# First layer of a three-layer network on one core: input loads moved behind their readiness, four gate buffers, elementwise products moved from GpSimd to VectorE

## The chip, the core and the metric

The kernel runs on one core of one Trainium2 chip. The metric is the device time of one execution in microseconds (us), lower is better. The core's engines are TensorE (PE; its weight loads are listed apart as PEld), VectorE (DVE), ScalarE (ACT), GpSimd (POOL) and SyncE (SP). They run side by side and wait for each other by semaphores. Transfers are issued by SP and by ScalarE here, each of which has a row of transfers of its own; the names SPq and ACTq in a row mean the issuing side of those engines.

## The reference

The network has three layers on x of 512 tokens by 1024 features: a time-mixing layer of the RWKV-7 kind, a layer of forgetting attention, and a hybrid sparse-attention layer, each followed by an MLP. The change lies in the first layer's time mixing, cut here to what it computes (h is the normalised input; 16 heads of 64):

```python
xs = h[None] + xx[None] * mu[:, None, None, :]      # six mixes of h and the token before
rkv = einsum('pbtd,pde->pbte', stack([x_r, x_k, x_v]), w_rkv)
w = -softplus(-(w0 + tanh(x_w @ w1) @ w2)) - 0.5;  decay = exp(-exp(w))
a = sigmoid(a0 + (x_a @ a1) @ a2)
g = sigmoid(x_g @ g1) @ g2                          # the gate
...
def step(S, inp):                                   # once per token, S is 64 x 64 per head
    sa = einsum('bhvk,bhk->bhv', S, -kk_t)
    S = S * w_t + sa[..., None] * b_t[:, :, None, :] + v_t[..., None] * k_t[:, :, None, :]
    return S, einsum('bhvk,bhk->bhv', S, r_t)
y = (y - mean) * rsqrt(var + GN_EPS)                # per head
y = y * lnx_w + lnx_b
y = (y + bonus) * g
return y @ w_o                                      # added to x by the caller
```

## The kernel before

Matrix products of the large layers are taken as three products of high and low parts: an operand is split into a rounded high part (`wh`, a ScalarE copy) and the remainder (`wl`, a subtraction on VectorE or GpSimd). The kernel is written as generators which are advanced in turn; a scheduler then orders each engine's instructions from those of all generators, and puts in the semaphores. Buffers come from pools by tag, so a tile waits until an older tile of its tag is no longer read. The first layer lasts until about 500 us of the trace; after it come its MLP and the other two layers.

The first layer's core goes through the 512 tokens in chunks of 64, and its work in halves: `T2` is the half of the tokens (256 each), `hs` the half of the heads, and `tt` one of four tiles of 128 tokens.

- `rwkv_gate` makes the gate: it mixes x again (`xh` buffers), multiplies by two small matrices, and writes 8 tiles `gst` (128x512) to memory, each by a ScalarE copy out of PSUM (L1147) and a store issued by ScalarE (L1148).
- `rwkv_prep` stores the scaled keys and queries into `dQ` in memory. `prepare(T2)` in `rwkv_core` reads them back (`KBg` at L1306, `Qd` and `Qe` at L1310), multiplies them (L1315) into 8 matrices `G` of 128x16x128, and masks each product (128x512, 32 in all). In the first half VectorE masks straight from PSUM; in the second half ScalarE copies every second product out of PSUM (L1320) and GpSimd masks it (L1322).
- `rwkv_inverse` inverts 32x32 triangles for all heads in 31 steps of two VectorE instructions (L1263, L1265), once for each half.
- `chain(hs)` carries the state through 8 chunks. After each tile of tokens `rwkv_post` normalises the result `y` (L1531 to L1542) with one product on GpSimd (L1540); TensorE then transposes it (L1546).
- `weight(k, ...)` loads the 8 row blocks of the output matrix and splits them, two 128x512 pieces each: high part on ScalarE (L1439), low part `wo` on GpSimd (L1440).
- `out(tt)` loads the layer's input x again for one tile of tokens (L1448, two loads of 128x4x128, 256 KB each), multiplies by the output matrix, and adds.

Of the kernel before, what the change touches and what calls it, by code (L numbers as in the profile page):

```python
# [9 lines left out]
F32 = mybir.dt.float32  # L10
# [3 lines left out]
ALU = mybir.AluOpType  # L14
# [4 lines left out]
P = 128  # L19
D = 1024  # L20
T = 512
# [10 lines left out]
class Net:  # L32
# [1072 lines left out]
    def rwkv_gate(self, e):  # L1105

        nc, a, pool, fv = self.nc, self.a, e["p7"], e["p2"]
        w = self.load_w(a["rw_g1"], 1280)
        Ms = (P, 32)
        ps = [self.bank("t") for _ in range(2)]  # L1110
        for m in range(NK):
            h, d = self.rwkv_again(e, pool, m, pool, "xd", 2)
            nc.vector.scalar_tensor_tensor(d, d, self.v("mu5", m), h[:, 1:], op0=ALU.mult, op1=ALU.add)
            xh, xl = self.split(pool, d, "xg", 2, lpool=m % 2 == 0)
            o = 160 * m
            for p, M in zip(ps, Ms):
                self.mm3(p[:M], w[0][:, o:o + M], w[1][:, o:o + M], xh, xl, m == 0, m == NK - 1)
                o += M
            yield
        sh, sl = [pool.tile([P, T], F32R, name=n) for n in ("sgh", "sgl")]  # L1120
        st = pool.tile([96, T], F32R, name="sgt")
        for i, M in enumerate(Ms):
            t = pool.tile([P, T], F32, tag="xd", bufs=2, name=self.nm("sg"))[:M]
            nc.scalar.activation(t, ps[i][:M], AF.Tanh, scale=0.5)
            nc.gpsimd.tensor_scalar(t, t, 0.5, 0.5, op0=ALU.mult, op1=ALU.add)
            if i == 0:
                nc.scalar.copy(sh, t)
                nc.vector.tensor_tensor(sl, t, sh.bitcast(F32), op=ALU.subtract)
            else:
                nc.scalar.copy(st[0:32], t)  # L1130
                nc.scalar.copy(st[32:64], t)
                nc.vector.tensor_tensor(st[64:96], t, st[0:32].bitcast(F32), op=ALU.subtract)
        gh, gl = [self.wp.tile([P, 2048], F32R, tag=t, bufs=2, name=self.nm(t)) for t in ("wh", "wl")]
        self.load_w(a["rw_g2"], 1024, dst=[gh[:, :1024], gl[:, :1024]])
        self.load_w(a["rw_g2t"], 1024, rows=96, dst=[gh[:, 1024:], gl[:, 1024:]])
        nc.vector.tensor_copy(gh[32:64, 1024:], gl[32:64, 1024:].bitcast(F32))
        for tt in range(4):
            b = slice(tt * P, (tt + 1) * P)
            for hf in range(2):
                o = slice(512 * hf, 512 * hf + 512)  # L1140
                ps = self.bank("acc")
                nc.tensor.matmul(ps, sh[:, b], gh[:, o], start=True, stop=False)
                nc.tensor.matmul(ps, sh[:, b], gl[:, o], start=False, stop=False)
                nc.tensor.matmul(ps, sl[:, b], gh[:, o], start=False, stop=False)
                nc.tensor.matmul(ps, st[:, b], gh[:96, 1024 + 512 * hf:1536 + 512 * hf], start=False, stop=True)
                t = fv.tile([P, T], F32, tag="vst", bufs=2, name=self.nm("gst"))
                nc.scalar.copy(t, ps)  # L1147
                nc.scalar.dma_start(e["g"][tt, :, o], t)  # L1148
            yield
# [119 lines left out]
    def rwkv_core(self, e):  # L1269

        nc, a, dp, fp = self.nc, self.a, e["dp"], e["pd"]
# [19 lines left out]
        def prepare(T2):  # L1291

            S = fp.tile([P, 32, 32], F32, tag="is", bufs=1, name=self.nm("is"))
            dq = nc.sync if T2 else nc.scalar
            gs = []
            for hs in range(2):
                if hs == 1 and T2 == 0:
# [2 lines left out]
                for u in range(2):  # L1300
                    g = G[T2, hs][u]
                    gs.append(g)
                    tt = 2 * T2 + u
                    kb = (e["pd2"] if T2 or hs else fp).tile([P, 2, 4, P], F32, tag="KBg", bufs=2 if T2 or hs else 1,
                                                             name=self.nm("KBg"))
# [5 lines left out]
                    for ev in range(2):  # L1311
                        for pp in range(2):
                            ps = self.bank(("o", "acc")[pp] if T2 else "s")
                            for p in (2 * pp, 2 * pp + 1):
                                nc.tensor.matmul(ps[:, p % 2 * 256:p % 2 * 256 + 256], kb[:, ev, p], kr[:, ev, p],  # L1315
                                                 start=True, stop=True)
                            o = 8 * ev + 4 * pp
                            src, eng = ps.rearrange("q (p t) -> q p t", t=P), nc.vector
                            if T2 and pp:
                                nc.scalar.copy(g[:, o:o + 4, :], src)  # L1320
                                src, eng = g[:, o:o + 4, :], nc.gpsimd
                            eng.tensor_tensor(g[:, o:o + 4, :], src, e["mask"][:, None, :].to_broadcast([P, 4, P]),  # L1322
                                              op=ALU.mult)

                        if len(BK[hs]) < 7:
                            tb = self.bank("t")
                            for p in range(4):
                                nc.tensor.transpose(tb[:, p * P:(p + 1) * P], kb[:, ev, p], self.ident)
                            pool = e["pc3"] if T2 else (fp, e.get("pd2"))[hs]
                            bk = pool.tile([P, 4, P], F32, tag="BK", bufs=6 if T2 else 4, name=self.nm("BK"))  # L1330
                            nc.scalar.mul(bk, tb.rearrange("q (p t) -> q p t", t=P), -1.0)
                            BK[hs].append(bk)
                        yield
# [16 lines left out]
            for g in gs:  # L1350
                nc.vector.transpose(yt[64:96].rearrange("p (h t) -> p h t", t=32), g[64:96, :, 0:32])
                W = self.bank("o")
                for h in range(16):
                    o = slice(h * 32, h * 32 + 32)
# [3 lines left out]
                for h in range(16):  # L1358
                    o = slice(h * 32, h * 32 + 32)
# [73 lines left out]
        def weight(k, h, l):  # L1433

            raw = self.wp.tile([P, 1024], F32, tag="wr", bufs=3, name=self.nm("wor"))
            nc.sync.dma_start(raw, a["rw_o"][k])
            for i in range(2):
                o = slice(512 * i, 512 * i + 512)
                nc.scalar.copy(h[:, o], raw[:, o])  # L1439
                nc.gpsimd.tensor_tensor(l[:, o], raw[:, o], h[:, o].bitcast(F32), op=ALU.subtract)  # L1440
            wo[k] = h, l

        def out(tt):

            b = slice(tt * P, tt * P + P)
            for hf in range(2):
                x = self.xall[:, 4 * hf:4 * hf + 4, b]
                nc.scalar.dma_start(x, a["x"][4 * hf:4 * hf + 4, :, b].rearrange("m p t -> p m t"))  # L1448
                ps, o = self.bank("o"), slice(512 * hf, 512 * hf + 512)
                for k in range(NK):  # L1450
                    hi, lo = [x[:, k % 4] for x in e["O"][tt, k // 4]]
# [3 lines left out]
                t = e["pc3"].tile([P, T], F32, tag="sc", bufs=self.nsc, name=self.nm("ot"))  # L1455
# [62 lines left out]
    def rwkv_post(self, fp, e, tt, hs, y):  # L1518

        nc, a = self.nc, self.a  # L1520
# [16 lines left out]
        nc.vector.tensor_scalar(st[:, 1], st[:, 1], 1.0 / 64, 64e-5, op0=ALU.mult, op1=ALU.add)  # L1537
        f = self.rsqrt(fp, st[:, 1], 8)
        nc.vector.tensor_tensor(h3(y), h3(y), bc(f), op=ALU.mult)
        nc.gpsimd.tensor_tensor(y, y, lnx[:, 0], op=ALU.mult)  # L1540
        nc.vector.tensor_tensor(y, y, v, op=ALU.add)
        nc.vector.tensor_tensor(y, y, gt, op=ALU.mult)  # L1542
        yield
# [132 lines left out]
```

## Time and profile before

| what | value |
|---|---|
| median of 3 runs | 2310.77 us (2310.65 to 2317.59) |
| profiled execution, its own time | 2310.41 us |
| span of its trace | 2308.7 us |
| PE busy | 2206.2 us (96%) |
| DVE busy | 1371.0 us (59%) |
| ACT busy | 942.0 us (41%) |
| POOL busy | 568.6 us (25%) |
| mean granted TensorE clock | 0.985 of full speed |

The span is the time from the first to the last instruction in the trace; 1.7 us of the execution's own time lie around it. Busy shares are means over the whole program, and its stages have different limits, so the rows below are taken by stretches of the span. In a row of waits, the engine and line that stood still come first, then what it waited for.

### The profile page before, as it was taken

Reading aid. Unit: us, or ns where it says so; the run is one execution under the profiler, and the core shown is the slowest. Engines: PE = TensorE matmul, PEld = TensorE weight load, DVE = VectorE, ACT = ScalarE, POOL = GpSimd, SP = SyncE. Lnnn points to the kernel's source line nnn. Section 1 sums busy time; section 2 is a strip of 40 time slices with the busy share of each in tenths; the row PEclk is TensorE's granted clock in tenths of the full one; section 3 lists DMA queues with packets and bytes.
Section 4 is the critical chain, followed back from the end, with each engine's and each line's share of the span. In section 5 each row is a group of like instructions: output and inputs, shape, how many; then the busy total and the mean of one; then the engine's idle time right before and its main releaser. Section 6 shows DMA issues by size and latency. Waiting matters only on the chain.

```text
span 2308.7 us, 32324 instructions
## 1 busy us (share of the span) xinstructions
PE 2206.2 (96%) x12161; PEld 1832.3 (79%) x12161; DVE 1371.0 (59%) x2718; ACT 942.0 (41%) x1928; POOL 568.6 (25%) x655
## 2 busy tenths in 40 slices
PE   4988777999999999999999999999999999999999
PEld 4768666878888889998788888898777788888887
DVE  8997868755444457876744444756664445444443
ACT  5574455433323345665523323344444324332331
POOL 6554335220120112444220120303322111112010
PEclk9998988999999999999999999999999999999999
DMA  3158633212232233332322223232222432232222
GB/s 124 41 159 251 176 104 127 75 38 92 93 105 95 92 102 109 102 101 72 108 99 98 92 93 107 75 113 79 92 88 100 132 122 97 91 103 99 92 92 82
DMA packets 104012, 237.32 MB, mean 103 GB/s; under 512 B 9664, under 2 KB 42176, under 8 KB 103856
## 3 DMA queue, kind: packets, MB, share of 16 engines
q1 hardware_dynamic: 73712, 214.28, 29.1%
q10 hardware_dynamic: 30144, 20.98, 3.1%
q8 instruction: 96, 1.57, 0.3%
q14 instruction: 60, 0.49, 0.1%
HBM read 210.02 MB, written 18.91 MB: 99 GB/s over the span
## 4 chain that ended last, share of the span: by engine, by line
PE 82%; DVE 6%; DMA 2%; ACT 1%; issue 1%; POOL 0%; ACTq 0%; SPq 0%; DVEq 0%; POOLq 0%
PE psacc L146 20%; PE psacc L149 20%; PE psacc L147 20%; PE psacc L266 3%; PE psacc L268 2%; PE psacc L267 2%; PE pso L378 2%; PE pst L368 1%; DVE wl L92 1%; DVE xgl L176 1%; PE pso L1452 1%; PE pso L1454 1%; PE pso L1453 1%; PE pss L747 0%; PE pss L748 0%
## 5 line engine op out<-in xcount | busy, mean ns | idle before, releaser
L91 ACT CAST wh<-wr 128x512 fp32r<-128x512 f32 (+1 forms) x593 | 323.6, 616 | 455.9 <-PE psacc L149 327.8
L92 DVE TENSOR_TENSOR wl<-wr,wh 128x512 fp32r<-128x512 f32 (+1 forms) x581 | 423.2, 781 | 33.9 <-ACT wh L91 31.0
L149 PE MATMUL psacc<-xgl,wh 128*128 128x512 f32 x1104 | 431.9, 392 | 2.3 <-DVE xgl L176 2.3
L146 PE MATMUL psacc<-xg,wh 128*128 128x512 f32 x1104 | 432.9, 392 | 0.0
L147 PE MATMUL psacc<-xg,wl 128*128 128x512 f32 x1104 | 432.2, 392 | 0.0
L146 PE MATMUL psacc<-hid,wh 128*128 128x512 f32 x768 | 299.7, 393 | 0.0
L149 PE MATMUL psacc<-hidl,wh 128*128 128x512 f32 x768 | 299.1, 392 | 0.0
L147 PE MATMUL psacc<-hid,wl 128*128 128x512 f32 x768 | 298.5, 391 | 0.0
L254 POOL TENSOR_TENSOR xall<-xall,yt 128x512 f32<-128x512 f32 x72 | 107.6, 1495 | 669.5 <-DVE yt L253 669.5
L149 PEld LDWEIGHTS psacc<-xgl,wh 128*128 128x128 f32 x1104 | 207.3, 188 | 46.6 <-DVE xgl L176 4.5
L147 PEld LDWEIGHTS psacc<-xg,wl 128*128 128x128 f32 x1104 | 207.4, 188 | 42.6 <-issue 0.8
L146 PEld LDWEIGHTS psacc<-xg,wh 128*128 128x128 f32 x1104 | 207.4, 188 | 41.8 <-ACT xg L175 0.2
L253 DVE TENSOR_TENSOR yt<-psacc,rb 128x512 f32<-128x512 f32 x96 | 66.4, 692 | 273.4 <-PE psacc L149 273.4
L241 DVE TENSOR_TENSOR ht<-ht,psacc 128x512 f32<-128x512 f32 x96 | 66.0, 688 | 225.3 <-ACT ht L240 225.2
L240 ACT ACTIVATE ht<-psacc 128x512 f32<-128x512 f32 x96 | 57.4, 598 | 283.4 <-PE psacc L149 283.3
L149 PEld LDWEIGHTS psacc<-hidl,wh 128*128 128x128 f32 x768 | 144.2, 188 | 32.7
L147 PEld LDWEIGHTS psacc<-hid,wl 128*128 128x128 f32 x768 | 144.2, 188 | 32.0
L146 PEld LDWEIGHTS psacc<-hid,wh 128*128 128x128 f32 x768 | 144.2, 188 | 31.4
L266 PE MATMUL psacc<-wh,xg 128*128 128x256 f32 (+2 forms) x504 | 144.6, 287 | 2.7 <-ACT gt L651 1.6
L268 PE MATMUL psacc<-wh,xgl 128*128 128x256 f32 (+2 forms) x504 | 143.9, 286 | 0.6 <-DVE gq L597 0.6
L267 PE MATMUL psacc<-wl,xg 128*128 128x256 f32 (+2 forms) x504 | 143.7, 286 | 0.0
L200 POOL TENSOR_TENSOR ssacc<-ssacc,sq 128x512 f32<-128x512 f32 x35 | 52.6, 1504 | 227.4 <-ACT sq L199 226.4
(492 smaller groups left out, 4011.1 us busy)
## 6 DMA issues: line engine op xcount, KB each, us to landing
wr<-in_mlp_in_dram SPq DMA_DIRECT2D x96, 512.0 KB, 4.2
wr<-in_mlp_out_dram SPq DMA_DIRECT2D x96, 512.0 KB, 4.2
dQ<-q ACTq DMA_DIRECT2D x8, 1024.0 KB, 6.3
wr<-in_w_q_dram SPq DMA_DIRECT2D x12, 512.0 KB, 3.8
wr<-in_rw_k_dram SPq DMA_DIRECT2D x8, 512.0 KB, 3.5
wr<-in_rw_r_dram SPq DMA_DIRECT2D x8, 512.0 KB, 3.3
wr<-in_rw_v_dram SPq DMA_DIRECT2D x8, 512.0 KB, 5.8
wor<-in_rw_o_dram SPq DMA_DIRECT2D x8, 512.0 KB, 3.5
```

Source lines behind the costliest of these rows:

```text
L91: nc.scalar.copy(h, r)
L92: (eng or nc.vector).tensor_tensor(wl[:rows, b:f], r, h.bitcast(F32), op=ALU.subtract)
L146: nc.tensor.matmul(ps_, wi[0], xh, start=i == 0, stop=False)
L147: nc.tensor.matmul(ps_, wi[1], xh, start=False, stop=False)
L149: nc.tensor.matmul(ps_, wi[0], xl, start=False, stop=i == n - 1)
L240: nc.scalar.activation(t, ps, AF.Relu)
L241: nc.vector.tensor_tensor(t, t, ps, op=ALU.mult)
L253: nc.vector.tensor_tensor(t, ps, r2, op=ALU.mult)
L254: (nc.vector if q == 3 else nc.gpsimd).tensor_tensor(self.xs[m], self.xs[m], t, op=ALU.add)
L266: nc.tensor.matmul(o, xh[:, b], wh, start=kt == 0, stop=False)
L267: nc.tensor.matmul(o, xh[:, b], wl, start=False, stop=False)
L268: nc.tensor.matmul(o, xl[:, b], wh, start=False, stop=kt == NK - 1)
```

## The change

Five edits, all in the first layer. (1) Four of the eight gate tiles `gst` are taken from the buffers of tag `xh`, so that there are four buffers and not two. (2) The loads of `KBg`, `Qd` and `Qe` of the first half are issued by SP instead of ScalarE, as those of the second half are. (3) All masks of `G` are products on VectorE straight from PSUM; ScalarE's copies and GpSimd's products for 8 of them are gone. (4) The 16 low parts of the output matrix and the 8 products of `rwkv_post` are computed on VectorE instead of GpSimd. (5) The 8 loads of x are issued by SP, and each stands behind a new GpSimd copy of one column that reads the normalised result `O` of its tile of tokens, so that it cannot start before that.

```diff
--- before.py
+++ after.py
@@ -1143,7 +1143,8 @@
                 nc.tensor.matmul(ps, sh[:, b], gl[:, o], start=False, stop=False)
                 nc.tensor.matmul(ps, sl[:, b], gh[:, o], start=False, stop=False)
                 nc.tensor.matmul(ps, st[:, b], gh[:96, 1024 + 512 * hf:1536 + 512 * hf], start=False, stop=True)
-                t = fv.tile([P, T], F32, tag="vst", bufs=2, name=self.nm("gst"))
+                t = (fv.tile([P, T], F32, tag="vst", bufs=2, name=self.nm("gst")) if hf else
+                     pool.tile([P, T + 1], F32, tag="xh", bufs=2, name=self.nm("gst"))[:, 0:T])
                 nc.scalar.copy(t, ps)
                 nc.scalar.dma_start(e["g"][tt, :, o], t)
             yield
@@ -1291,7 +1292,7 @@
         def prepare(T2):
 
             S = fp.tile([P, 32, 32], F32, tag="is", bufs=1, name=self.nm("is"))
-            dq = nc.sync if T2 else nc.scalar
+            dq = nc.sync
             gs = []
             for hs in range(2):
                 if hs == 1 and T2 == 0:
@@ -1315,12 +1316,8 @@
                                 nc.tensor.matmul(ps[:, p % 2 * 256:p % 2 * 256 + 256], kb[:, ev, p], kr[:, ev, p],
                                                  start=True, stop=True)
                             o = 8 * ev + 4 * pp
-                            src, eng = ps.rearrange("q (p t) -> q p t", t=P), nc.vector
-                            if T2 and pp:
-                                nc.scalar.copy(g[:, o:o + 4, :], src)
-                                src, eng = g[:, o:o + 4, :], nc.gpsimd
-                            eng.tensor_tensor(g[:, o:o + 4, :], src, e["mask"][:, None, :].to_broadcast([P, 4, P]),
-                                              op=ALU.mult)
+                            nc.vector.tensor_tensor(g[:, o:o + 4, :], ps.rearrange("q (p t) -> q p t", t=P),
+                                                    e["mask"][:, None, :].to_broadcast([P, 4, P]), op=ALU.mult)
 
                         if len(BK[hs]) < 7:
                             tb = self.bank("t")
@@ -1437,7 +1434,7 @@
             for i in range(2):
                 o = slice(512 * i, 512 * i + 512)
                 nc.scalar.copy(h[:, o], raw[:, o])
-                nc.gpsimd.tensor_tensor(l[:, o], raw[:, o], h[:, o].bitcast(F32), op=ALU.subtract)
+                nc.vector.tensor_tensor(l[:, o], raw[:, o], h[:, o].bitcast(F32), op=ALU.subtract)
             wo[k] = h, l
 
         def out(tt):
@@ -1445,7 +1442,9 @@
             b = slice(tt * P, tt * P + P)
             for hf in range(2):
                 x = self.xall[:, 4 * hf:4 * hf + 4, b]
-                nc.scalar.dma_start(x, a["x"][4 * hf:4 * hf + 4, :, b].rearrange("m p t -> p m t"))
+
+                nc.gpsimd.tensor_copy(x[:, 0, 0:1], e["O"][tt, 0][0][:, 0, 0:1].bitcast(F32))
+                nc.sync.dma_start(x, a["x"][4 * hf:4 * hf + 4, :, b].rearrange("m p t -> p m t"))
                 ps, o = self.bank("o"), slice(512 * hf, 512 * hf + 512)
                 for k in range(NK):
                     hi, lo = [x[:, k % 4] for x in e["O"][tt, k // 4]]
@@ -1537,7 +1536,7 @@
         nc.vector.tensor_scalar(st[:, 1], st[:, 1], 1.0 / 64, 64e-5, op0=ALU.mult, op1=ALU.add)
         f = self.rsqrt(fp, st[:, 1], 8)
         nc.vector.tensor_tensor(h3(y), h3(y), bc(f), op=ALU.mult)
-        nc.gpsimd.tensor_tensor(y, y, lnx[:, 0], op=ALU.mult)
+        nc.vector.tensor_tensor(y, y, lnx[:, 0], op=ALU.mult)
         nc.vector.tensor_tensor(y, y, v, op=ALU.add)
         nc.vector.tensor_tensor(y, y, gt, op=ALU.mult)
         yield
```

Over the whole program PE has 11007 instructions before and after, DVE 2720 and now 2752, ACT 1862 and 1834, POOL 660 and 636, SP 522 and 542. Line numbers of the changed kernel lie one higher than before from L1147 to L1318 and three lower from there to L1445, and one lower after that.

The first place is the issuing side of ScalarE in the first half of the core (`dQ`, `dV` and `KBg` are tiles of memory and loads from it, `BK` and `vst` copies of the core and of the values). Before:

```order
L1448 DMA xall<-in_x_dram 128x4x128
L1254 COPY bon<-pso_1583 128x4x2
L1448 DMA xall<-in_x_dram 128x4x128
L1331 ACTIVATE BK_1726<-pst_1721 128x512
L1306 DMA KBg_1738<-dQ_80 128x1024
L1247 DMA dQ_81<-q_1575 2048x1x128
L1448 DMA xall<-in_x_dram 128x4x128
L1170 COPY vst_1954<-psacc_1929 128x256
L1448 DMA xall<-in_x_dram 128x4x128
L1171 DMA dV<-vst_1954 128x256
```

Now:

```order
L1255 COPY bon<-pso_1583 128x4x2
L1328 ACTIVATE BK_1726<-pst_1721 128x512
L1171 COPY vst_1926<-psacc_1901 128x256
L1172 DMA dV<-vst_1926 128x256
L1171 COPY vst_1954<-psacc_1929 128x256
L1248 DMA dQ_81<-q_1575 2048x1x128
L1172 DMA dV<-vst_1954 128x256
L1248 DMA dQ_81<-q_1601 2048x1x128
```

The loads of `xall` and of `KBg` have left this row; the stores of `dQ` and `dV` stay. SP's row at the same place has weight loads (`wr`) and the input for the gate (`xh`). Before:

```order
L86 DMA wr_2035<-in_rw_v_dram 128x1024
L86 DMA wr_2187<-in_rw_v_dram 128x1024
L86 DMA wr_2193<-in_rw_v_dram 128x1024
L86 DMA wr_2433<-in_rw_g_dram 128x1024
L1099 DMA xh_1869<-in_x_dram 128x512
L1099 DMA xh_1985<-in_x_dram 128x512
L1099 DMA xh_2125<-in_x_dram 128x512
L86 DMA wr_2439<-in_rw_g2t_dram 96x1024
```

Now:

```order
L86 DMA wr_2035<-in_rw_v_dram 128x1024
L86 DMA wr_2187<-in_rw_v_dram 128x1024
L1307 DMA KBg_1738<-dQ_80 128x1024
L86 DMA wr_2193<-in_rw_v_dram 128x1024
L86 DMA wr_2433<-in_rw_g_dram 128x1024
L1099 DMA xh_1869<-in_x_dram 128x512
L1099 DMA xh_1985<-in_x_dram 128x512
L1307 DMA KBg_2008<-dQ_81 128x1024
L1307 DMA KBg_2274<-dQ_81 128x1024
L1311 DMA Qd_1685<-dQ_81 64x8x128 x2
L1311 DMA Qe_2004<-dQ_81 64x8x128 x2
L1099 DMA xh_2125<-in_x_dram 128x512
```

The first `KBg` load stands behind two weight loads and ahead of the next. The loads of `KBg`, `Qd` and `Qe` from the second memory tile stand between the second and the third load of `xh`.

The second place is VectorE in the first inversion (`it` and `iy` are its two tiles), whose steps stand between the masks of `G` of the second half. Before:

```order
L1263 TENSOR_TENSOR it_2679<-ix_2677,iy_2678 128x256
L1265 TENSOR_TENSOR iy_2678<-iy_2678,it_2679 128x16x16
L1263 TENSOR_TENSOR it_2679<-ix_2677,iy_2678 128x255
L1265 TENSOR_TENSOR iy_2678<-iy_2678,it_2679 128x17x15
L1263 TENSOR_TENSOR it_2679<-ix_2677,iy_2678 128x252
L1265 TENSOR_TENSOR iy_2678<-iy_2678,it_2679 128x18x14
L1263 TENSOR_TENSOR it_2679<-ix_2677,iy_2678 128x247
L1322 TENSOR_TENSOR G_2531<-pso_2537,mask 128x512
```

Now:

```order
L1264 TENSOR_TENSOR it_2671<-ix_2669,iy_2670 128x256
L1319 TENSOR_TENSOR G_2531<-pso_2537,mask 128x512
L1319 TENSOR_TENSOR G_2531<-psacc_2541,mask 128x512
L1319 TENSOR_TENSOR G_2531<-psacc_2556,mask 128x512
L1319 TENSOR_TENSOR G_2532<-psacc_2577,mask 128x512
L1266 TENSOR_TENSOR iy_2670<-iy_2670,it_2671 128x16x16
L1319 TENSOR_TENSOR G_2531<-pso_2552,mask 128x512
L1264 TENSOR_TENSOR it_2671<-ix_2669,iy_2670 128x255
```

Four masks, three of them out of the `psacc` buffers that ScalarE and GpSimd served, now stand together ahead of the step on 16x16, where one stood seven rows further on.

The third place is VectorE at the end of the second inversion (`ib` is its transposed result), where the first tile `y` of `rwkv_post` ends (the last `Qe` row of a `y` is L1542 before and L1541 now). Before:

```order
L1539 TENSOR_TENSOR y_2937<-y_2937,rsz_3243 128x512
L1265 TENSOR_TENSOR iy_2962<-iy_2962,it_2963 128x31
L1541 TENSOR_TENSOR y_2913<-y_2913,Qe_2004 128x512
L1343 STREAM_TRANSPOSE ib_3323<-iy_2962 128x1024
L1542 TENSOR_TENSOR y_2913<-y_2913,Qe_2004 128x512
L1347 COPY G_2531<-ib_3323 32x32x16
L1347 COPY G_2532<-ib_3323 32x32x16
```

Now:

```order
L1189 TENSOR_TENSOR rst_3236<-rsz_3235 128x8
L1344 COPY G_2598<-ib_3315 32x32x16
L1344 COPY G_2599<-ib_3315 32x32x16
L1408 TENSOR_TENSOR Z_2899<-Z_2899,pc 64x2x64 x2
L1348 STREAM_TRANSPOSE YT_1687<-G_2531 32x512
L1540 TENSOR_TENSOR y_2905<-y_2905,Qe_2004 128x512
L1190 TENSOR_TENSOR rst_3236<-rst_3236,gn_3227 128x8
L1437 TENSOR_TENSOR wo_3739<-wor_3791,wo_3738 128x512 x2
L1437 TENSOR_TENSOR wo_3778<-wor_3779,wo_3777 128x512
L1541 TENSOR_TENSOR y_2905<-y_2905,Qe_2004 128x512
L1191 SCALAR_TENSOR_TENSOR rsz_3235<-rst_3236,rsz_3235 128x8
L1437 TENSOR_TENSOR wo_3778<-wor_3779,wo_3777 128x512
```

L1542 of the first `y` (number 2913) stood one row behind the transpose. Now its last row (L1541 of number 2905) stands behind copies into `G`, rows of `rwkv_post`, and three of the `wo` products; ten of the sixteen `wo` products stand ahead of this stretch, and so does the transpose.

## Rows read from the trace of the kernel before

**Rows 1.** Windows: stretch, length, busy PE, PEld, DVE, ACT, POOL, granted clock, DMA share, GB/s.

```profile
160.00:204.00 44.00, 39.65 (x252) 35.46 (x251) 43.74 (x53) 29.33 (x58) 27.43 (x31) 0.93 0.78 225
204.00:217.00 13.00, 7.90 (x44) 6.90 (x44) 6.05 (x10) 2.48 (x7) 2.60 (x5) 0.76 0.96 287
217.00:260.00 43.00, 42.07 (x279) 37.05 (x277) 29.09 (x38) 17.45 (x32) 18.51 (x21) 0.99 0.75 210
260.00:268.00 8.00, 2.75 (x10) 1.16 (x9) 5.74 (x9) 3.59 (x5) 0.39 (x1) 0.86 0.69 195
268.00:322.00 54.00, 38.22 (x201) 30.07 (x200) 39.61 (x81) 30.05 (x43) 20.15 (x24) 0.82 0.57 166
322.00:386.00 64.00, 48.65 (x697) 42.12 (x696) 55.99 (x157) 27.00 (x63) 19.70 (x19) 0.85 0.22 67
386.00:500.00 114.00, 110.59 (x1113) 90.45 (x1112) 71.54 (x209) 45.06 (x97) 35.03 (x30) 0.97 0.25 80
500.00:2308.00 1808.00, 1792.96 (x9025) 1492.75 (x9024) 978.86 (x1979) 691.93 (x1456) 356.36 (x431) 1.00 0.30 97
```

**Rows 2.** Waits of PE, 204 to 386: total us, times, longest.

```profile
PE psacc L1546 <- DVE y L1542: 10.2, 1, 10.2
...
PE pss L1315 <- DMA KBg<-dQ: 5.0, 1, 5.0
PE psacc L1315 <- ACT gst L1147: 4.4, 1, 4.4
PE pst L134 <- DVE xgl L160: 3.0, 1, 3.0
```

**Rows 3.** ScalarE, timeline from 205: start, us, row, idle before and its releaser.

```profile
205.16 0.48 ACTq L1306 DMA_DIRECT2D KBg<-dQ  x1
...
206.32 7.16 ACTq L1448 DMA_DIRECT2D xall<-in_x_dram  x1
213.52 0.37 ACT L1170 COPY vst<-psacc 128x256 f32<-128x256 f32 x1 [7.79 <-DMA KBg<-dQ]
```

**Rows 4.** Waits of DVE, 204 to 330.

```profile
DVE G L1322 <- PE pso L1315: 9.6, 4, 7.5
...
DVE wl L92 <- ACT wh L91: 7.1, 2, 7.0
DVE ix L1340 <- ACT is L1335: 4.5, 2, 2.2
```

**Rows 5.** Tile `gst`: ScalarE's idle time before its rows, and its stores.

```profile
  DMA dg<-gst: 9.8, 5
...
DMA to landing us min/median/max: 2.0/2.6/6.0
```

**Rows 6.** Groups, POOL then DVE, 285 to 500: count, busy, mean ns, idle before.

```profile
L1440 POOL TENSOR_TENSOR wo<-wor,wo 128x512 fp32r<-128x512 f32 x16 | 21.5, 1363 | 7.5 <-ACT wo L1439 6.6 <-DVE gn L1531 0.8
L1540 POOL TENSOR_TENSOR y<-y,Qd 128x512 f32<-128x512 f32 x8 | 11.9, 1504 | 47.9 <-DVE rsz L1190 23.3 <-DVE rst L1189 21.5 <-DVE y L1539 3.1
L1322 POOL TENSOR_TENSOR G<-G,mask 128x512 f32<-128x512 f32 x8 | 10.2, 1284 | 7.6 <-ACT G L1320 7.4
```
```profile
L1322 DVE TENSOR_TENSOR G<-pso,mask 128x512 f32<-128x512 f32 x8 | 5.5, 689 | 9.7 <-PE pso L1315 9.6
```

**Rows 7.** Timeline of DVE and POOL: one drawn-out DVE row and its neighbours.

```profile
378.35 0.16 DVE L1190 SCALAR_TENSOR_TENSOR rsz<-rst,rsz 128x8 f32<-128x8 f32 x1
...
379.75 2.58 POOL L1440 TENSOR_TENSOR wo<-wor,wo 128x512 fp32r<-128x512 f32 x2
...
381.14 1.22 DVE L1190 SCALAR_TENSOR_TENSOR rsz<-rst,rsz 128x8 f32<-128x8 f32 x1
```

**Rows 8.** SP, timeline from 202; then DMA issues 190 to 330: count, KB, us to landing.

```profile
202.82 1.93 SPq L86 DMA_DIRECT2D wr<-in_rw_v_dram  x2
```
```profile
KBg<-dQ SPq DMA_DIRECT2D x4, 512.0 KB, 4.2
KBg<-dQ ACTq DMA_DIRECT2D x3, 512.0 KB, 7.4
```

## Prediction

> **What bounds the kernel now.** I read the windows by stage first [rows 1]. From 500 us to the end TensorE is busy for 1793 of 1808 us, and no edit reaches there; from 386 to 500 it is busy for 110.6 of 114. What can be won lies before 386, where each stage has another limit. From 160 to 204 VectorE has no idle time (43.74 of 44). I call the next stretches A (204 to 217, TensorE busy for 7.9 of 13), B (217 to 268: nearly full up to 260, then 2.75 of 8), C (268 to 322: 38.2 of 54) and D (322 to 386: 48.7 of 64, while VectorE is busy for 56).
>
> Then the waits of TensorE, which say what was late in each [rows 2]: in A a `KBg` load (5.0), in B a split on VectorE (3.0), in C a gate copy that held a PSUM bank (4.4), in D the last product on the first `y` (10.2). Last the timeline of ScalarE, which stands behind the first and the third of them: at 206.32 its issue of one x load lasted 7.16 us, and its next work began at 213.52 [rows 3]. VectorE stood still for a ScalarE copy queued behind that (7.0) [rows 4].
>
> **The change part by part.**
>
> *x loads and `KBg` off ScalarE's row (A).* ScalarE no longer stands from 206.3 to 213.5. The `KBg` load was issued there at 205.16, and by the row at 213.52 it landed at about 213.5, 8.4 later [rows 3]; the median of such loads on that row is 7.4, on SP's it is 4.2 [rows 8]. On SP the load stands behind two weight loads, which were issued from 202.82 to 204.75 [rows 8]. With an issue at about 204.8 and 4.2 it lands at 209.0, some 4.5 earlier. The x loads (8 of 256 KB) are no longer read around A, where transfers are 96% busy [rows 1], and VectorE's wait for ScalarE ends with the long issue. I take 5.0, the whole wait for `KBg`. Bounds: 1 (SP's row is about as late as ScalarE's) and 8.8 (VectorE's 7.0, and 7.9 us of TensorE's work at B's clock of 0.99 instead of 0.76, worth 1.8).
>
> The Trainium skill ("DMA: Bandwidth & Descriptors", section "Issuing engines are not separate DMA queues") says that transfers share the same 16 DMA engines whichever engine starts them, and that spreading them over several issuers only saves issue time. By it alone A would win nothing and the sum below would be 11 instead of 16; the row of 7.16 us is issue time, though, and so just what by this rule can be saved.
>
> *The gate's input and its splits (B).* The third of the 8 `xh` loads now stands behind six loads of the core in SP's row, which wait for the stores to `dQ`. The 3.0 for a split go if ScalarE and VectorE come 5 earlier out of A, and stay if `xh` is late. I take 2.0, nearer to the first, as the `dQ` stores come earlier too; bounds 0 and 3.0.
>
> *Gate buffers (C).* ScalarE stood for 9.8 ahead of five `gst` copies until a store had landed (median 2.6, once 6.0) [rows 5]. TensorE, in order, stood for 4.4 behind one of these copies [rows 2], and then VectorE's longest idle time in the first inversion began: 7.5 for the product L1315 [rows 4]. With four buffers a copy waits for the store four tiles back and not two; of a store that takes 6.0, two copies of some 0.6 and their products leave little uncovered, and I put the rest at 1.2. So C gains 7.5 less 1.2 = 6.3. The 2.2 that the inverse's input waits for ScalarE's copies `is` [rows 4] go too, since ScalarE loses 8 copies ahead of them: 8.5.
>
> *Masks (C).* VectorE takes 8 masks at 0.689, the row of its own 8 masks of the same shape and source: 5.5. GpSimd loses 8 products at 1.284 [rows 6]. Against the 5.5 stands what GpSimd's products cost VectorE. In the timeline I count 15 rows of VectorE between 295 and 386 that last longer than the same row does elsewhere, each beside a GpSimd product; the last is `rsz` on 128x8, 1.22 beside 0.16 alone [rows 7]. Their excess is 16.3 us: 6.0 in the five rows of C, 10.3 in the ten of D. Without masks on GpSimd C gets its 6.0 back, so the edit gives 0.5, and the sum for C is 9.0. Bounds: 3 (the masks, which now stand ahead of the inversion's steps, cost their 5.5 on the path) and 14 (7.5, 2.2 and the 4.4 all go).
>
> *Low parts and `y` products (D).* 10 of the 16 `wo` products stand ahead of the second inversion's end on VectorE. At the 0.689 of a product of that shape they are 6.9, and one `y` product 0.7, against 10.3 of relief: VectorE wins 2.7. But the first `y`, for which TensorE waited 10.2, stands about 13 rows behind the transpose and not one. I take 0 for D; bounds 4 won (the relief and some clock, now 0.85) and 5 lost.
>
> *After 386 (E).* Six `wo` and seven `y` products, 13 x 0.689 = 9.0, come to a VectorE that is busy for 71.5 of 114; TensorE at 97% hides them. If that cover is gone, the 9.0 are on the path, less the 0.8 by which each `y` product is shorter than GpSimd's 1.504 [rows 6], 3.4 in all. The x loads now wait on SP for a GpSimd copy of one column, which waits for `O`; the trace has no such row, and GpSimd is idle for 79 of 114 us. Behind them in SP's row are weight loads of the MLP, which wait for buffers anyway. A 256 KB load of 4 to 8 us (the 512 KB `KBg` took 4.2 and 7.4) lies under the 24 products of its own tile with 512 columns. I take 0; bounds 0 and 3.4 lost.
>
> Sum: 5.0 + 2.0 + 9.0 + 0 + 0 = 16.0. The profiled execution took 2310.41 (the median of the runs is 0.36 higher); 2310.4 - 16.0 = 2294.4.
>
> **The rivals.**
>
> R1, VectorE gives back a part. A, B and C win as above, but in D VectorE is the limit, 56 of 64, and 13 rows delay the first `y` by 7 while TensorE waits (0.54 each, my estimate between 0.16 and 0.69, the short and the long rows above, nearer to the long). For it: the 10.2 [rows 2] are a wait for VectorE. Against it: the ten drawn-out rows of D. 2294.4 + 7 = 2301.4.
>
> R2, SP's row is the new queue. `KBg` lands no earlier behind 1 MB of weights, the `xh` loads wait behind loads that wait for `dQ`, A wins nothing, and B loses 2 instead of winning 2. For it: the 96% in A [rows 1]. Against it: SP's `KBg` loads landed faster than ScalarE's [rows 8]. 2294.4 + 5 + 4 = 2303.4. The Trainium skill (the same page, "Queues, rings and completion order") has the DMA engines serve the queue rows in turn; by it one row gets a smaller share than two, which speaks for this rival, and the 4.2 beside 7.4 speak against.
>
> R3, the change does not do what it says: gate stores and `KBg` wait for memory, not for buffers or order, so the waits of A and C stay under other names. About 2 of issue time are won: 2308.4.
>
> R4, slower. The drawn-out rows stay, because GpSimd's remaining products (those on `v` in the post) draw them out as well, and VectorE gets 32 products x 0.689 = 22 more, 13 of it (8 masks, 10 `wo`, one `y`) in C and D, where it is late already. Less A's 5: 2310.4 + 13 - 5 = 2318.4. It decides if less than about 3 of the 16.3 are relieved and VectorE's idle 7.5 in C stays.
>
> **How the numbers follow.** The forecast has 0.52, R1 0.22, R2 0.13, R3 0.08, R4 0.05. The range goes from 2283 (A, B and C at about nine tenths of their upper bounds, D at 3) to 2306 (R2 with a third of R1's 7), and leaves out R3, R4 and a little at the lower end. 0.3% of the time, 6.9 us, is about what a measurement of this kernel can tell from no change, so faster begins below 2303.9. The forecast lies there nearly whole (0.50), R1 mostly (0.19), R2 by half (0.07), R3 hardly (0.01): 0.77. Slower has R4 and a tail of R2: 0.06; 0.17 are left for the same.
>
> **What would show it.** A: no ScalarE issue above 1 us between 200 and 217, and less than 1 of waiting for `KBg` on TensorE. B: no wait of VectorE for `xh` that is longer than before. C: `gst` copies waiting for `dg` for 1.2 or less, VectorE's longest idle time in the first inversion below 2, 16 masks of the second half at 0.69. D: fewer than three drawn-out rows up to the end of the second inversion, and a wait for the first `y` within 5 of 10.2. The point from which TensorE is full, 386 before, should come near 370, and all later rows be shifted by that. The forecast is wrong if TensorE waits for a load in SP's row for more than 5, if VectorE is full through C, or if x loads are among TensorE's waits behind 386.

## The result and the profile after

The changed kernel is faster: its runs lie between 2298.25 and 2303.41 us, those of before between 2310.65 and 2317.59; the ratio is 0.9947, with a 95% interval of 0.9936 to 0.9958. The profiled execution took 2298.25 instead of 2310.41, which is 12.2 less, and its span is 2296.5. The forecast was 16.0 less, 2294.4, in a range of 2283 to 2306. The ratio gives about 12.3 less, with 9.7 to 14.8 for its interval; the medians, 2312.61 and 2302.56, lie 10.05 apart. The profiled execution of the changed kernel is the fastest of its five, so a difference of a few us in one stage of one pair of profiles is not safe by itself.

First the windows of the changed kernel over the same stretches as [rows 1], with the same columns (length, busy time of PE, PEld, DVE, ACT and POOL, granted clock, DMA share, GB/s):

```profile
204.00:217.00 13.00, 10.54 (x80) 9.78 (x79) 10.82 (x18) 4.27 (x10) 7.85 (x7) 1.00 0.87 261
268.00:322.00 54.00, 35.39 (x232) 29.59 (x231) 43.48 (x94) 23.23 (x31) 10.40 (x14) 0.78 0.55 156
322.00:386.00 64.00, 54.01 (x756) 47.12 (x756) 56.34 (x164) 32.60 (x72) 6.68 (x10) 0.85 0.32 101
386.00:500.00 114.00, 110.95 (x1044) 90.83 (x1045) 75.70 (x217) 45.88 (x100) 18.34 (x24) 0.99 0.28 89
```

A changed as forecast (TensorE 10.5 of 13, before 7.9). C did not: TensorE is busy for less of it, not more. Fixed stretches compare different work, though, once one trace runs ahead. So here are the two traces cut at the same points of the work: the first gate copy, the end of the first inversion, the start and the end of the second, the third tile of `rwkv_post`, and the last addition to x. Before:

```profile
204.00:274.40 70.40, 59.12 (x356) 50.43 (x356) 46.40 (x71) 27.59 (x50) 22.31 (x27) 0.90 0.74 211
274.40:308.40 34.00, 25.04 (x110) 19.32 (x109) 24.32 (x56) 16.63 (x26) 11.54 (x14) 0.90 0.76 215
308.40:320.40 12.00, 5.65 (x46) 4.29 (x44) 8.21 (x9) 8.93 (x11) 6.28 (x7) 0.72 0.27 92
320.40:383.70 63.30, 49.36 (x712) 42.83 (x712) 55.30 (x155) 26.41 (x62) 20.00 (x20) 0.85 0.20 64
383.70:397.90 14.20, 12.26 (x167) 10.86 (x168) 9.69 (x19) 10.27 (x17) 11.78 (x10) 0.70 0.70 224
397.90:506.60 108.70, 104.67 (x978) 84.37 (x976) 67.29 (x200) 39.90 (x88) 24.48 (x22) 1.00 0.20 64
```

Changed:

```profile
204.00:269.20 65.20, 57.95 (x364) 49.48 (x363) 47.31 (x73) 28.23 (x51) 25.33 (x29) 0.95 0.73 211
269.20:308.50 39.30, 27.09 (x122) 22.11 (x121) 30.16 (x65) 17.05 (x23) 8.53 (x12) 0.87 0.75 214
308.50:313.70 5.20, 0.14 (x3) 0.17 (x4) 4.86 (x7) 3.84 (x4) 1.87 (x2) 0.50 0.00 0
313.70:369.90 56.20, 50.83 (x734) 44.35 (x734) 48.86 (x156) 25.57 (x60) 3.12 (x6) 0.86 0.23 72
369.90:392.60 22.70, 16.74 (x221) 14.77 (x219) 17.93 (x37) 11.99 (x21) 6.39 (x7) 0.69 0.58 187
392.60:496.10 103.50, 100.45 (x932) 81.91 (x932) 69.47 (x206) 38.76 (x86) 14.00 (x19) 1.00 0.25 77
```

The reader is to take the differences of the second column: -5.2, +5.3, -6.8, -7.1, +8.5, -5.2, in sum -10.5. The remaining 1.7 of the 12.2 lie behind the core, where the same rows took 1802.1 and 1800.4; over all profiles here that stretch took 1798.3 to 1804.8, so those 1.7 say nothing. Of the 10.5, 7.6 are less idle time of TensorE (46.5 to 38.9) and 2.9 less busy time (256.1 to 253.2 for nearly the same number of matmuls, 2369 and 2376; the mean granted clock is 0.91 in both).

The waits of TensorE in the changed kernel, 204 to 386, name what came in place of [rows 2]:

```profile
PE pso L1352 <- DVE YT L1348: 17.4, 2, 12.1
PE pso L1316 <- DVE G L1319: 4.3, 3, 3.4
PE pss L1316 <- issue: 2.4, 1, 2.4
```

The waits for the gate copy and the first `y` are gone. The wait for `KBg` has shrunk from 5.0 to the 2.4 that the list gives as "issue": it ended at 210.54 with the first product on `KBg`, and that load had landed at 210.45. The two waits for `YT` stand behind the two inversions:

```profile
313.56 1.89 PE L1352 MATMUL pso<-YT,G 128*32 128x32 f32 x32 [12.11 <-DVE YT L1348]
376.12 1.92 PE L1352 MATMUL pso<-YT,G 128*32 128x32 f32 x32 [5.30 <-DVE YT L1348]
```

Behind the first inversion TensorE has run out of other work and stands for 12.1, until VectorE has finished the inversion and transposed its first result. Before, it stood there for 5.3, for a mask that came behind the inversion, and behind the second inversion for the 10.2 of [rows 2], where now 5.3 are left:

```profile
PE pso L1315 <- DVE G L1322: 5.9, 2, 5.3
```

The gate tile `gst` as in [rows 5]:

```profile
  DMA dg<-gst: 1.2, 1
...
DMA to landing us min/median/max: 2.5/4.9/6.2
```

ScalarE's wait of 9.8 became 1.2, exactly the size forecast. But the first inversion ends no earlier, and the timeline of VectorE inside it shows new waits. GpSimd waits for a gate store beside it, as it did before (6.8 then):

```profile
277.61 0.69 DVE L1319 TENSOR_TENSOR G<-pso,mask 128x512 f32<-128x512 f32 x1 [0.88 <-DMA dg<-gst]
278.22 1.28 DVE L1319 TENSOR_TENSOR G<-psacc,mask 128x512 f32<-128x512 f32 x2
283.21 0.69 DVE L1319 TENSOR_TENSOR G<-psacc,mask 128x512 f32<-128x512 f32 x1 [3.71 <-DMA dg<-gst]
```
```profile
283.90 1.46 POOL L1377 MEMSET VS<- 64x512 f32 x3 [4.76 <-DMA dg<-gst]
```

A mask now waits 3.71 for a gate store. The product in PSUM was done by 281.3; what the mask lacked is its target, since `G` of the second half lies in a pool (`pc3`) that is opened on the memory of the gate's pools, and the two new gate buffers are in that memory: the store that this mask waited for is the seventh, from one of them, and it landed at 283.0. The order of VectorE with its waits shows it, the same mask before and in the changed kernel (the DMA names are the semaphores of transfers):

```order
L1322 TENSOR_TENSOR G_2532<-pso_2575,mask 128x512 [waits PE_49,Activation_49]
```
```order
L1319 TENSOR_TENSOR G_2532<-psacc_2577,mask 128x512 [waits DMAHW1_49,DMAHW5_49,PE_49,Activation_49]
```

The wait has moved from ScalarE's copy into VectorE's row, and behind it in that row stand the steps of the inversion.

### The profile page after: what moved, and what is told of

Same layout as the page of the kernel before. It is cut to its first block, busy times and chain, and to the rows that moved or that the text cites. A ratio compares the mean times of both kernels' runs of the same rounds, so it can differ in the third digit from the quotient of the medians.

```text
span 2296.5 us, 32348 instructions
## 1 busy us (share of the span) xinstructions
PE 2202.6 (96%) x12161; PEld 1832.5 (80%) x12161; DVE 1377.8 (60%) x2750; ACT 937.6 (41%) x1920; POOL 530.1 (23%) x631
## 4 chain that ended last, share of the span: by engine, by line
PE 84%; DVE 10%; DMA 2%; ACT 2%; issue 1%; SPq 0%; POOL 0%; ACTq 0%; DVEq 0%
PE psacc L146 21%; PE psacc L147 21%; PE psacc L149 20%; PE psacc L266 3%; PE psacc L268 3%; PE psacc L267 3%; PE pso L378 2%; PE pst L368 1%; DVE wl L92 1%; DVE mix L1003 1%; DVE xgl L176 1%; PE pso L1451 1%; PE pso L1452 1%; PE pso L1453 1%; PE pso L1352 1%
```

## The experiments

Single executions of one kernel differ here by several us (those of before, over all runs, from 2305.65 to 2323.17), so the ratios, with their intervals, decide, and the profiles say where. "Core end" is the start of the last addition to x in the profiled execution; "drawn out" counts rows of VectorE between 320 and 390 that last over 0.3 us longer than the shortest of the same row in any of the kernels, with their summed excess.

| kernel | ratio (95%) | first gate copy | end of inversions | core end | drawn out |
|---|---|---|---|---|---|
| before | 1 | 274.4 | 308.4, 383.7 | 506.6 | 10, 10.5 us |
| changed | 0.9947 (0.9936 to 0.9958) | 269.2 | 308.5, 369.9 | 496.1 | 2, 1.4 us |
| e1, x early | 0.9956 (0.9942 to 0.9969) | 273.9 | 313.9, 376.8 | 504.4 | 0 |
| e2, core loads on ScalarE | 0.9948 (0.9935 to 0.9960) | 266.8 | 307.3, 368.6 | 495.4 | 0 |
| e3, two gate buffers | 0.9944 (0.9932 to 0.9957) | 270.8 | 307.7, 371.5 | 496.5 | 1, 1.0 us |
| e4, masks shared | 0.9946 (0.9934 to 0.9959) | 267.2 | 302.4, 374.6 | 496.7 | 2, 1.4 us |
| e5, low parts and y on GpSimd | 0.9976 (0.9966 to 0.9986) | 268.1 | 308.2, 369.3 | 501.1 | 14, 12.1 us |
| e10, low parts on GpSimd | 0.9975 (0.9965 to 0.9986) | 269.3 | 309.5, 370.6 | 504.6 | 16, 13.4 us |
| e11, y on GpSimd | 0.9958 (0.9942 to 0.9974) | 268.2 | 308.3, 371.7 | 497.4 | 1, 1.1 us |
| e6, before + x late | 0.9990 (0.9977 to 1.0003) | 272.1 | 304.5, 386.3 | 511.2 | 12, 11.3 us |
| e7, before + low parts, y | 0.9990 (0.9979 to 1.0000) | 276.8 | 310.5, 384.5 | 508.6 | 2, 1.8 us |
| e8, before + x late + low parts, y | 0.9956 (0.9939 to 0.9972) | 273.3 | 305.6, 387.7 | 505.9 | 3, 2.2 us |
| e9, before + the other three edits | 0.9985 (0.9975 to 0.9995) | 270.7 | 312.5, 372.4 | 503.9 | 15, 12.3 us |
| e12, before + masks + low parts, y | 0.9969 (0.9954 to 0.9983) | 276.2 | 313.0, 383.3 | 505.5 | 1, 0.4 us |

**e1.** The changed kernel, edit 5 undone:

```diff
-                nc.gpsimd.tensor_copy(x[:, 0, 0:1], e["O"][tt, 0][0][:, 0, 0:1].bitcast(F32))
-                nc.sync.dma_start(x, a["x"][4 * hf:4 * hf + 4, :, b].rearrange("m p t -> p m t"))
+                nc.scalar.dma_start(x, a["x"][4 * hf:4 * hf + 4, :, b].rearrange("m p t -> p m t"))
```

> The changed kernel with the 8 x loads back on ScalarE's row and early. Theory (the x loads stop ScalarE in stage A and that is the gain of A): ScalarE shows an issue of some 7 us again near 206, the first gate copy comes about 5 us later, ratio to before 0.997. Rival (A was won by moving KBg to SP's row alone): no such loss, ratio 0.9947 as the changed kernel.

One part of the theory held: the first gate copy came 4.7 later, and the core end 8.3 later, in this execution (the slowest of its five). But over the runs the loss is 0.0009, inside the interval, which speaks for the rival. No ScalarE issue above 3 us came back, so here it was not a stuck row that made the stage late. TensorE waits for another load of the core:

```profile
PE pss L1316 <- DMA Qd<-dQ: 5.0, 1, 5.0
```

It is as long as the wait for `KBg` in [rows 2]. The core's loads land later with the x loads beside them, on SP's row too; the rows are under e2.

**e2.** The changed kernel, edit 2 undone:

```diff
-            dq = nc.sync
+            dq = nc.sync if T2 else nc.scalar
```

> The changed kernel with the KBg, Qd and Qe loads of the first half back on ScalarE's row, the x loads still late. Theory (with the x loads gone ScalarE's row is as good as SP's): first gate copy within 1 us of the changed kernel's 269.2, ratio 0.9947 within 0.0006. Rival (SP's row lands KBg 4 us earlier and that is A's gain): KBg lands 3 to 4 us later, ratio 0.996 to 0.997.

The theory held by the ratio; the first gate copy is 2.4 earlier in this execution, not within 1. The load that A waits for is the first `KBg` load. The last number is the time in us from its issue to its landing, in this order: before, the changed kernel, e1, e2, e6.

```profile
KBg<-dQ ACTq DMA_DIRECT2D x1, 512.0 KB, 8.4
KBg<-dQ SPq DMA_DIRECT2D x1, 512.0 KB, 5.6
KBg<-dQ SPq DMA_DIRECT2D x1, 512.0 KB, 7.1
KBg<-dQ ACTq DMA_DIRECT2D x1, 512.0 KB, 3.5
KBg<-dQ ACTq DMA_DIRECT2D x1, 512.0 KB, 3.8
```

With the x loads late, ScalarE's row, with 7.4 the slower in [rows 8], lands this load sooner than SP's, where it stands behind two weight loads. The two medians that my term A compared were of loads at different times. The later loads differ: the median of the three on ScalarE's row is 4.7 in e2 but 6.8 in e6, without an x load beside them in either; why is open.

**e3.** The changed kernel, edit 1 undone:

```diff
-                t = (fv.tile([P, T], F32, tag="vst", bufs=2, name=self.nm("gst")) if hf else
-                     pool.tile([P, T + 1], F32, tag="xh", bufs=2, name=self.nm("gst"))[:, 0:T])
+                t = fv.tile([P, T], F32, tag="vst", bufs=2, name=self.nm("gst"))
```

> The changed kernel with two gate buffers. Theory (the buffers are a gain of their own): ScalarE waits some 9 us for gate stores again, the first inversion ends 4 to 6 us later, ratio 0.9965 to 0.9975. Rival (the masks of the second half wait for the last gate store anyway, so the four buffers only move the wait): the inversion ends within 2 us of 308.5, ratio 0.9947 within 0.0006.

The rival held, though not in all of its words: the masks don't wait for a store here, but for TensorE, which waits for ScalarE. The last gate copy comes at 286.0 instead of 276.8 and ScalarE waits 9.7 for stores again, yet the first inversion ends at 307.7, no later than with four buffers, and the ratio is the same. VectorE's longest wait inside it:

```profile
286.04 0.69 DVE L1318 TENSOR_TENSOR G<-psacc,mask 128x512 f32<-128x512 f32 x1 [4.71 <-PE psacc L1315]
```

4.7 for the product with two buffers, 4.6 (0.88 and 3.71) for the stores with four: in these two executions the buffers move a wait and remove none.

**e4.** The changed kernel, edit 3 undone:

```diff
-                            nc.vector.tensor_tensor(g[:, o:o + 4, :], ps.rearrange("q (p t) -> q p t", t=P),
-                                                    e["mask"][:, None, :].to_broadcast([P, 4, P]), op=ALU.mult)
+                            src, eng = ps.rearrange("q (p t) -> q p t", t=P), nc.vector
+                            if T2 and pp:
+                                nc.scalar.copy(g[:, o:o + 4, :], src)
+                                src, eng = g[:, o:o + 4, :], nc.gpsimd
+                            eng.tensor_tensor(g[:, o:o + 4, :], src, e["mask"][:, None, :].to_broadcast([P, 4, P]),
+                                              op=ALU.mult)
```

> The changed kernel with 8 masks of the second half back on ScalarE and GpSimd. Theory (the first inversion is VectorE's, and the 10 masks that came into it, 6.9 us, took C's gain): it ends about 4 us before 308.5, less what GpSimd's products draw out (3 us), ratio 0.9930 to 0.9947. Rival (as I predicted, the masks on VectorE are paid for by undisturbed rows): it ends at 308.5 or later, ratio 0.995 to 0.997.

Its place is confirmed, its worth is none: the first inversion ends 6.1 earlier (302.4; 2.0 of that is there at the first gate copy), but the second ends 4.7 later, and the time is the same. The windows of e4 from the start of the second inversion to its end, and from there to the third tile of `rwkv_post`:

```profile
310.30:374.60 64.30, 53.49 (x747) 46.66 (x748) 53.12 (x169) 27.35 (x64) 3.12 (x6) 0.82 0.23 75
374.60:386.10 11.50, 8.94 (x87) 7.65 (x85) 11.05 (x20) 7.18 (x12) 4.62 (x5) 0.55 0.70 227
```

What was won up to 302 is in the longer second inversion (64.3, with 11.2 of VectorE idle, against 56.2 with 7.3). What made it longer is not shown.

**e5, e10, e11.** The changed kernel with edit 4 undone, in e5 both lines, in e10 the first alone, in e11 the second:

```diff
-                nc.vector.tensor_tensor(l[:, o], raw[:, o], h[:, o].bitcast(F32), op=ALU.subtract)
+                nc.gpsimd.tensor_tensor(l[:, o], raw[:, o], h[:, o].bitcast(F32), op=ALU.subtract)
...
-        nc.vector.tensor_tensor(y, y, lnx[:, 0], op=ALU.mult)
+        nc.gpsimd.tensor_tensor(y, y, lnx[:, 0], op=ALU.mult)
```

> The changed kernel with the 16 low parts and 8 y products back on GpSimd. Theory (the second inversion got 14 us shorter because GpSimd no longer draws out VectorE's rows): ten or so drawn-out rows come back, the time from the end of the first inversion to the end of the second is 70 us or more (61.4 in the changed kernel), ratio 0.9965 to 0.9975. Rival (the stretch got shorter because masks and waits left it, and the 24 products cost VectorE as much as they free): 61 to 65 us, ratio 0.9945 or less.

> The changed kernel with the 16 low parts of the output matrix back on GpSimd, the y products left on VectorE. Theory (the low parts draw out VectorE's rows between 320 and 390, ten or more of them, and TensorE's work of that stretch slips behind 390): ratio 0.9965 to 0.9975. Rival (the y products on the way to the output are what counts): ratio 0.9947 within 0.0006.

> The changed kernel with the 8 y products back on GpSimd, the low parts left on VectorE. Theory (the low parts are what counts): ratio 0.9947 to 0.9955. Rival (the y products, 0.8 us longer each on GpSimd and on the way to the output): ratio 0.9965 to 0.9975.

The low parts are the largest single term: without them on VectorE the ratio goes from 0.9947 to 0.9976 and 0.9975, about 6.5 us; the y products alone do nothing that can be told apart (0.9958). The theory's place was wrong: in e5 the drawn-out rows are back, 14 of them, but the stretch from the first inversion's end to the second's is 61.1, as in the changed kernel (61.4). There the 10 low parts that stand on VectorE cost about what the drawn-out rows cost. The loss is behind it. In e5, timeline of VectorE, then of GpSimd:

```profile
377.72 1.25 DVE L1190 TENSOR_TENSOR rst<-rst,gn 128x8 f32<-128x8 f32 x1
379.50 1.23 DVE L1191 SCALAR_TENSOR_TENSOR rsz<-rst,rsz 128x8 f32<-128x8 f32 x1
381.99 1.19 DVE L1190 TENSOR_TENSOR rst<-rst,gn 128x8 f32<-128x8 f32 x1
```
```profile
377.68 5.48 POOL L1437 TENSOR_TENSOR wo<-wor,wo 128x512 fp32r<-128x512 f32 x4 [5.11 <-ACT wo L1436]
```

These are the rows of [rows 7] in the same place: small rows of the reciprocal root of `rwkv_post`, on the way to the output, each nearly as long as one of the four GpSimd products beside them (5.48 in all). In the changed kernel the row `rsz` at 379.19 takes 0.16. From the second inversion's end to the last addition e5 took 131.8, e10 134.0, the changed kernel 126.2. What TensorE waits for there is plainest in e10, from 366 on:

```profile
PE psacc L1545 <- DVE y L1541: 6.6, 2, 3.7
```

The changed kernel has no wait for `y` there. In e9, where the masks are on VectorE and the low parts on GpSimd too, it is 6.35. In e5 it is only 1.3, beside 2.8 for `Z` on VectorE and 2.6 for a load, so there the loss is not all of this kind.

**e6, e7, e8.** The kernel before with edit 5 alone, with edit 4 alone, and with both (the lines as shown above and in the diff of the change).

> The kernel before with only the x loads moved to SP and behind O. Theory (stage A is the x loads): first gate copy 4 to 6 us before 274.4, ratio 0.9975 to 0.998. Rival (they are worth something only with KBg on SP's row): ratio 0.999 to 1.000.

> The kernel before with only the low parts and y products on VectorE. Theory (relief of the drawn-out rows in D): the same stages up to the end of the first inversion, then 6 to 10 us won up to the end of the second, half of it kept at the end, ratio 0.9975. Rival (VectorE is the limit of D and the products cost what they free): ratio 0.9995 to 1.002.

> The kernel before with two edits only: x loads late on SP, and low parts and y products on VectorE. Theory (these two make the gain together, and the gate buffers, the core loads on SP and the masks add nothing): ratio to before 0.9940 to 0.9960, core at its end near 497 where the changed kernel has 496.1. Rival (each edit is worth about 0.1% and the gain is their sum): ratio 0.9975 to 0.9985.

Each alone gives 0.1%, hardly more than nothing; both give 0.44%, most of the change. For e6 the rival held. e7 lies between the two, nearer its rival: up to the second inversion's end it won 1.6 from the first gate copy on, not 6 to 10. For e8 the theory held by its ratio, though the core end in its profile (505.9, in its slowest execution, 2307.19 against a median of 2302.98) missed the 497.

**e9.** The kernel before with edits 1 to 3: 0.15%.

> The kernel before with the other three edits: four gate buffers, core loads on SP's row, all masks on VectorE. Theory (nothing, since the masks fill the first inversion and the x loads still stop ScalarE): ratio 0.999 to 1.001. Rival (sum of edits): ratio 0.9965 to 0.998.

Between theory and rival, and its interval ends below 1.

**e12.** The kernel before with edits 3 and 4, which take all these products off GpSimd:

> The kernel before with the products alone moved: masks, low parts and y products on VectorE, while the x loads stay early, the core loads on ScalarE and the gate buffers two. It tells apart why the low parts alone gave 0.1% and together with the late x loads 0.44%. Theory (the low parts need the masks gone from GpSimd as well, or the x loads gone; with the masks gone the gain is there): ratio to before 0.996 to 0.9975. Rival (they need the late x loads, whose row on ScalarE stands in front of the same work): ratio 0.9985 to 1.000.

The theory held: 0.31% with the x loads as early as before. So the low parts on VectorE pay when either the masks have left GpSimd as well or the x loads have left ScalarE. The intervals of e7 and e12 touch, though (0.9979 to 1.0000 and 0.9954 to 0.9983), and why the low parts gave only 0.1% in e7, where the drawn-out rows were gone too, stays open.

## Why the prediction was right, and where its terms were wrong

The direction and the range held; 12.2 came instead of 16.0. All figures of stages are of one execution of each kernel.

**A and B, 7.0 forecast, 5.2 measured** up to the first gate copy. SP issued the `KBg` load at 204.81 (forecast 204.8), and TensorE's product on it began at 210.54 instead of 213.6:

```profile
204.81 0.39 SPq L1307 DMA_DIRECT2D KBg<-dQ  x1
```
```profile
210.54 1.53 PE L1316 MATMUL pss<-Qd,KBg 128*128 128x256 f32 x6 [2.44 <-issue]
```

That is 3.1 of my 5.0 for A: the load took 5.6 and not 4.2, and of TensorE's wait for it 2.4 are left, against my mark of less than 1. The reason given was wrong in part: SP's row is not the faster one, and what counts for the first `KBg` load is the x transfers that run at the same time (8.4 and 7.1 us with them, 3.5 to 5.6 without). The rule of the Trainium skill ("DMA: Bandwidth & Descriptors", section "Issuing engines are not separate DMA queues"), that transfers run on the same engines whoever issues them, agrees with the load being late beside the x loads from either row; I had counted the 7.16 of issue time as what it lets one save, but in e1 no such row came back and the load was late all the same. B gave the other 2.1, as forecast, though not by its mark: VectorE's wait for `xh`, 7.8 before, is 9.6 now, and its longest 5.1 instead of 4.5. Its wait for a split (7.1 in all) fell to 1.3. ScalarE still has an issue of 3.83 at 213.31 (a store of `dV`), against my mark of at most 1.

**C, 9.0 forecast, 1.5 won:** 5.3 lost up to the end of the first inversion, 6.8 won from there to the start of the second, where C ended in my cut. This is the step that failed: "So C gains 7.5 less 1.2". VectorE's wait of 7.5 did go, and came back as 4.6 for the gate stores' memory and 3.2 in four waits for TensorE. I had not looked at what the masks' targets wait for, only at what ScalarE's copies do. And all 16 masks of the second half lie inside the first inversion, where six on VectorE did (two more stood behind it): 10 x 0.69 = 6.9, more than the 5.5 of my term. Their relief did not come there either, because the products on `v`, which R4 named, moved up beside the last steps: in the timeline of the changed kernel

```profile
303.09 1.00 DVE L1266 TENSOR_TENSOR iy<-iy,it 128x112 f32<-128x112 f32 x1
304.12 1.28 DVE L1264 TENSOR_TENSOR it<-ix,iy 128x87 f32<-128x87 f32 x1
305.44 0.97 DVE L1266 TENSOR_TENSOR iy<-iy,it 128x87 f32<-128x87 f32 x1
306.44 1.28 DVE L1264 TENSOR_TENSOR it<-ix,iy 128x60 f32<-128x60 f32 x1
```
```profile
302.86 1.10 POOL L1527 TENSOR_TENSOR Qe<-Qe,bon 128x512 f32<-128x512 f32 x1 [17.50 <-DMA Qe<-dV]
304.04 1.26 POOL L1528 TENSOR_TENSOR Qe<-Qe,Qd 128x512 f32<-128x512 f32 x1
```

These four rows of VectorE, the last of them 1.28 where it took 0.22 before, are 3.6 longer than the shortest of their kind. The 6.8 behind the inversion are two masks and waits for TensorE and for `is` copies, which are now over before, and four copies into `G`, which a GpSimd mask drew out (4.89 before, 2.90 now). Over the whole of C VectorE is idle for 4.0 less and busy for 2.5 more, which leaves the 1.5. What R1 says of D, TensorE waiting for VectorE, came in C: the wait behind the first inversion grew from 5.3 to 12.1. It is 11.5 to 12.2 in all seven kernels with four gate buffers and all masks on VectorE, 9.0 in e3 and 8.1 in e4, which undo the one or the other.

**D, 0 forecast, 2.8 won,** from the start of the second inversion (320.4 and 313.7) to where TensorE is full again. That point, 386 before, came at 376.1 and not near 370. The exchange of relief for low parts, 10.3 for 7.6, is the part that was sized well: it left 2.7 for VectorE, and the drawn-out rows of D fell from ten to two.

**E, 0 forecast, 1.0 won** from there to the last addition (121.0 before, 120.0 now). In the windows above the last two stretches show 8.5 lost and 5.2 won, but that is mostly the same work on the other side of the cut: TensorE is busy for 16.7 of the changed kernel's stretch ahead of the third tile, before for 12.3, and for 100.5 behind it, before for 104.7. E's added VectorE work was hidden, as I had counted. The 8 x loads cost nothing, as forecast: none is among TensorE's waits behind 386, and they landed in 3.3 in the median:

```profile
xall<-in_x_dram SPq DMA_DIRECT2D x8, 256.0 KB, 3.3
```

So the stages gave 5.2, 1.5, 2.8 and 1.0, 10.5 in all, against 7.0, 9.0, 0 and 0. C's missing 7.5 were made up for by half in D and E, which I had put at nothing, and the 1.7 behind the core say nothing; that the total came within 4 of the forecast is in part luck. By the runs, edits 4 and 5 alone give 0.9956 where all five give 0.9947; I had put them at 0 in D and E and at a part of A's 5. Edits 1 to 3, of which 1 and 3 carried C, add 0.0009 to these two, less than the intervals can tell from nothing. Edits 1 to 4 without the late x loads (e1) give 0.9956 as well. So the low parts are needed (0.9975 without them in e10), and beside them either the late x loads or the other edits; how these work together is open.

## What to carry to other kernels

The list of waits gives sums and not places: the timeline tells behind which inversion TensorE stood. A wait that ends with a buffer has a second candidate in line: before counting it as won, look at what the next user of the memory waits for (here the pool opened on the gate's memory), and at what stands behind that user in its engine's row. Products on GpSimd cost VectorE most here where its rows were small and in a chain; counting drawn-out rows stretch by stretch found the edit that mattered, but the gain showed in the stage after. Edits that each move 0.1% alone need runs of pairs: two of them gave 0.44% together, and each taken out of the whole gave another picture than each put in alone.

## What the runs showed of the hardware

A VectorE row on 128x8 took 1.2 us beside a GpSimd product of 1.3 and 0.16 without one; it happened not only to products of two tensors but also to a row with a scalar operand, before, beside a `wo` product that ran from 352.41:

```profile
352.41 2.82 POOL L1440 TENSOR_TENSOR wo<-wor,wo 128x512 fp32r<-128x512 f32 x2 [0.78 <-DVE gn L1531]
352.57 1.24 DVE L1532 TENSOR_SCALAR gn<-gn 128x8 f32<-128x8 f32 x1
```

And the first 512 KB `KBg` load landed 6.9 to 8.4 us after its issue in the five kernels with early x loads (before, e1, e7, e9, e12), and 3.5 to 6.1 in the nine with late ones: 3.5 to 3.8 from ScalarE's row (e2, e6, e8), 5.6 to 6.1 from SP's, behind two weight loads.
